# Residue-ordered query copies for the dilated heads, bias tables from memory, and gather buffers zeroed once

## The chip, the cores and the metric

The kernel runs on one core of one Trainium2 chip. The metric is the device time of one execution in microseconds (us), lower being better. The core's engines are TensorE (PE: matmuls, with its weight loads shown apart as PEld), VectorE (DVE), ScalarE (ACT), GpSimd (POOL) and SyncE (SP), which issues most of the DMAs. Each engine runs its own instructions in order and waits for the others by semaphores.

## The reference

One encoder block over 1024 tokens of width 1024: RMS norm, a combined projection to queries, keys and values, eight dilated heads and eight neighbourhood heads of width 64, an output projection, and a mixture of 16 experts with two chosen per token. What concerns the change is the dilated attention, whose bias depends on the head alone, and the gather of tokens for the experts:

```python
DIL_PATTERNS = ((128, 1), (512, 4), (2048, 16))

def dilated_window_attention(q, k, v, slopes, window, dilation):
    '''Centred dilated sliding window: query t attends to t + j*dilation, |j*dilation| <= window/2.
    Keys are gathered by stride: the sequence is split into `dilation` residue subsequences,
    each handled as a banded window of radius (window/2)/dilation over 64-query blocks.
    ...
    dist = (off * dilation).astype(jnp.float32)

    s = jnp.einsum('bhrnqd,bhrnkd->bhrnqk', qb, kb).astype(jnp.float32) * (HEAD_DIM ** -0.5)
    s = s - slopes[None, :, None, None, None, None] * dist
    s = jnp.where(valid, s, NEG_INF)
    ...

def dilated_mixture_attention(q, k, v, slopes):
    '''All (window, dilation) patterns per head, merged by their softmax denominators.'''
    results = [dilated_window_attention(q, k, v, slopes, w, d) for (w, d) in DIL_PATTERNS]
    ...
```

with slopes 2^-1, 2^-2, ... 2^-8 for the eight heads.

## The kernel before

Matmul operands are kept as two halves, a rounded high part (made by ScalarE, L103) and the remainder (made by VectorE or GpSimd, L104), and products are summed over the halves. The program goes through these stages, in the times of the profile: value projections (0 to 130 us); four pairs of dilated heads (130 to 345); four pairs of neighbourhood heads (345 to 480); the start of the output projection (480 to 545); its rest and the routing (545 to 620); the experts (620 to 892).

A pair of heads (class `Dil`, number `n` 0 to 3) has two heads `h`, and each head eight steps. Steps 0 to 3 are dense: the queries are 128 consecutive tokens. Steps 4 to 7 are residue steps: step 4 + r takes the tokens congruent to r modulo 4, in two halves z of 128 queries. The queries of a head lie as `q_s`, 128 partitions x 1024 tokens of 4 bytes, in the order of the tokens; the keys lie by residue already, since the evacuation that writes them (`k_hh`, L401) reads PSUM at a stride of 4. In `scores` (L411) the queries are the matmul's weights, so a residue step loads 128 weights with 16 bytes between them. Each half makes two matmuls (keys' high and low part), a step thus four: a score group.

The main loop (L852 on) goes through the steps s of all heads in one row, and the order in which it is written is the order on each engine. In step s it issues: the scores and biased softmax inputs of step s (`first`; `soft`, VectorE, L424); some projection matmuls of the next pair (`take`, L378, 96 in a pair, spread over its steps, the filling of TensorE); at step 1 and 2 of a pair the merge of the pair before (L578 among it); the transposes of step s-2 (`second`, L509) and their split into `pt_hi` (ScalarE) and `pt_lo` (VectorE); the exponentials of step s (`run_exps`, ScalarE, L430); up to two waiting evacuations of the projection (`run_slow(2)`: ScalarE L401, VectorE L402); at step 3 the store of the pair before (transposes of `ot`, L594); the value matmuls of step s-3 (`third`, L534 and L545), with `fold` (ScalarE, L438) and `ot` (VectorE, L440 or L442) after every second step. In residue steps `ot` is written at a stride of 4, in dense ones contiguously.

The biases of a head, 128 x 768, are made by GpSimd: at first `dist` and `mask` are loaded (`early_loads`, L459 and L460); for each head `prepare`, called in step 6 of the head before, halves `dist` (L465) and adds the mask to it (L466). GpSimd also splits weights (`w_lo`, L104). `early_loads` of the next head is called in step 1, and `late_loads` (the second copy `vb` of the values) in step 2.

For the experts, GpSimd gathers rows of tokens by an indirect DMA (`gather`, L1357) into the tiles `xg` and `xg1` (L1360); rows whose index is out of bounds are not written. The indices `gi` come from the routing.

Of the kernel before, what the change touches and what calls it, by code (L numbers as in the profile page):

```python
# [9 lines left out]
F32 = mybir.dt.float32  # L10
# [20 lines left out]
def shape_constants():  # L31

    p = np.arange(128)
# [11 lines left out]
    mask = -8 * np.concatenate([m_a, m_b], 1).astype(np.float32)  # L45

# [22 lines left out]
    return {"dist": dist, "mask": mask, "na_mask": na_mask, "ident": np.eye(128, dtype=np.float32),  # L69
# [3 lines left out]
def build(nc, tc, a, ctx, dbg=None):  # L73
# [71 lines left out]
    with ExitStack() as att:  # L145
# [15 lines left out]
        factors = qk.tile([128, 2], F32, name="factors", bufs=1)  # L161
# [11 lines left out]
        with ExitStack() as ph:  # L173
# [125 lines left out]
            nc.vector.memset(factors[:, 0:1], 0.5)  # L299
            nc.vector.memset(factors[:, 1:2], 8.0)  # L300
# [37 lines left out]
        class Pair:  # L338
# [70 lines left out]
            def scores(self, ps, h, qs, keys):  # L409
                for n, k in enumerate((self.kh, self.kl)):  # L410
                    nc.tensor.matmul(ps, self.q[h][:, qs], keys(k[h]), start=n == 0, stop=n == 1)  # L411
# [39 lines left out]
        class Dil(Pair):  # L451
# [3 lines left out]
            def early_loads(self, h):  # L455
                if self.n == 0 and h == 0:
                    Dil.dist = ap.tile([128, 768], F32, name="dist", tag="dist", bufs=1)
                    Dil.mask = ap.tile([128, 896], F32, name="mask", tag="mask", bufs=1)[:, :768]
                    nc.sync.dma_start(Dil.dist, a["dist"])  # L459
                    nc.sync.dma_start(Dil.mask, a["mask"])  # L460

            def prepare(self, h):
                head = 2 * self.n + h
                bias = self.bias[h] = ap.tile([128, 896], F32, name="bias", tag="bias")
                nc.gpsimd.tensor_tensor(Dil.dist, Dil.dist, factors[:, 0:1].to_broadcast([128, 768]), op=ALU.mult)  # L465
                nc.gpsimd.tensor_tensor(bias[:, :768], Dil.dist, Dil.mask, op=ALU.add)  # L466
# [7 lines left out]
            def late_loads(self, h):  # L474
                head = 2 * self.n + h
                vb = self.vb[h] = ap.tile([128, 8, 128], F32R, name="vb", tag="vb", bufs=1)
                nc.sync.dma_start(f(vb), vb_d[:, head * 128:(head + 1) * 128].rearrange("(k p) x -> p k x", p=128))

            def first(self, h, n):
# [4 lines left out]
                for z in range(2):  # L484
# [6 lines left out]
                    else:  # L491
                        r = n - 4
                        qs = slice(512 * z + r, 512 * z + r + 509, 4)
                        keys = lambda k: k[:, r * 256:r * 256 + 256]
                        todo.append((2 * r + z, 2, 512 - 128 * z))
                    self.scores(sp[:, 256 * z:256 * z + 256], h, qs, keys)
# [67 lines left out]
            def merge2(self):  # L564
# [5 lines left out]
                sb = ap.tile([128, 2, 2, 8], F32, name="sb")  # L570
                nc.vector.tensor_copy(sb.rearrange("p h z (q k) -> p k (h z) q", k=4),
                                      pb[:, 0:32].rearrange("p (k x q) -> p k x q", k=4, q=2))
                e = ap.tile([128, 2, 2, 8], F32, name="e")
# [793 lines left out]
    for e in range(2):  # L1367
        x0[e] = new_x()
        gather(x0[e], gi[:, 0, at(e)])
# [450 lines left out]
```

## Time and profile before

| | |
|---|---|
| median of 3 runs | 895.49 us (895.33 to 896.38) |
| profiled execution | 894.3 us |
| its span, first to last instruction | 892.5 us |
| mean granted clock of TensorE | 0.977 |
| busy in the span | PE 834.3 us (93%), DVE 565.1 (63%), ACT 512.6 (57%), POOL 234.4 (26%) |

A row of a timeline gives the start in microseconds from the span's start, the duration, the engine, the line, the operation, its output and inputs with their shapes, and in brackets how long the engine had been idle before and what ended that. Matmuls are pipelined: a row's duration is longer than what it adds, and what a row costs TensorE's queue is read from the start of the next. In a table by stage each engine has its busy time and its number of instructions in parentheses.

### The profile page before, as it was taken

The numbers are of one execution on the slowest core, as the hardware profiler recorded it, in microseconds if no ns is written. First come the engines' busy times: TensorE is split into PE (matmuls) and PEld (weight loads), VectorE is DVE, ScalarE is ACT, GpSimd is POOL, SyncE is SP. The second block draws the span as 40 slices with busy tenths as digits, with TensorE's granted clock in tenths as the row PEclk, the third lists the DMA queues.
The fourth block names the chain that finished last, engine by engine and source line by source line (L and its number), as shares of the span: only waits on it lengthen the run. The fifth ranks groups of instructions, "written<-read, shape, count | busy, mean of one in ns | idle before, by whom it ended". The sixth has DMA issues, their size and how long they took to land. (4 is left out here: it accounts for less than half of the span.)

```text
span 892.5 us, 13330 instructions
## 1 busy us (share of the span) xinstructions
PE 834.3 (93%) x4492; PEld 695.0 (78%) x4492; DVE 565.1 (63%) x1255; ACT 512.6 (57%) x1082; POOL 234.4 (26%) x187
## 2 busy tenths in 40 slices
PE   8999999999999999999898999999799999999962
PEld 5888878979889888878787887887677877777741
DVE  4551126776767767666677754677786566858693
ACT  5441127757667576677576623543585665857652
POOL 4001122221232202332310100000443343734553
PEclk8999999999999999999999999998999999999985
DMA  6865452314344141534447747995798987999743
GB/s 238 278 217 162 126 160 65 100 52 108 94 138 105 53 138 48 148 103 117 79 157 206 254 154 248 360 323 213 250 317 248 293 233 226 361 299 304 217 180 129
DMA packets 129919, 167.30 MB, mean 187 GB/s; under 512 B 15222, under 2 KB 101750, under 8 KB 129824
## 3 DMA queue, kind: packets, MB, share of 16 engines
q1 hardware_dynamic: 119616, 142.53, 49.6%
q0 software_dynamic: 10224, 23.79, 9.8%
q8 instruction: 41, 0.67, 0.3%
q14 instruction: 38, 0.31, 0.1%
HBM read 129.93 MB, written 47.47 MB: 199 GB/s over the span
## 5 line engine op out<-in xcount | busy, mean ns | idle before, releaser
L103 ACT ACTIVATE pt_hi<-ps_pt 128x512 fp32r<-128x512 f32 (+2 forms) x128 | 67.6, 528 | 70.6 <-PE ps_pt L509 41.5
L378 PE MATMUL ps_mm<-xhi,w_lo 128*128 128x512 f32 x256 | 105.1, 411 | 1.1 <-POOL w_lo L104 1.1
L378 PE MATMUL ps_mm<-xlo,w_hi 128*128 128x512 f32 x256 | 105.0, 410 | 0.0
L378 PE MATMUL ps_mm<-xhi,w_hi 128*128 128x512 f32 x256 | 102.9, 403 | 0.0
L104 POOL TENSOR_TENSOR w_lo<-w_raw,w_hi 128x1024 fp32r<-128x1024 f32 x16 | 38.3, 2394 | 229.3 <-ACT w_hi L103 229.3
L104 DVE TENSOR_TENSOR pt_lo<-ps_pt,pt_hi 128x512 fp32r<-128x512 f32 (+2 forms) x128 | 77.2, 603 | 31.8 <-ACT pt_hi L103 31.2
L424 DVE CUSTOM_DVE_ANT_0 p<-ps_s,bias 128x256 f32<-128x256 f32 (+1 forms) x192 | 81.8, 450 | 18.2 <-PE ps_s L411 10.8
L104 DVE TENSOR_TENSOR g_lo<-raw_up,g_hi 128x1024 fp32r<-128x1024 f32 x64 | 75.4, 1220 | 24.6 <-ACT g_hi L103 24.6
L1413 PE MATMUL ps_mm<-g_hi,x_hi 128*128 128x512 f32 x184 | 75.4, 410 | 0.9 <-ACT x_hi L103 0.9
L1413 PE MATMUL ps_mm<-g_hi,x_lo 128*128 128x512 f32 x184 | 74.0, 402 | 1.8 <-DVE x_lo L104 1.8
L1357 POOL DMA_INDIRECT xg<-hn_d,gi x32 | 44.3, 1383 | 118.0 <-ACT ge L1078 81.7
L1413 PE MATMUL ps_mm<-g_lo,x_hi 128*128 128x512 f32 x184 | 73.3, 398 | 0.0
L430 ACT ACTIVATE p<-p,stats 128x256 f32<-128x256 f32 x128 | 63.7, 500 | 9.7 <-DVE stats L424 9.5
L103 ACT ACTIVATE g_hi<-raw_up 128x1024 fp32r<-128x1024 f32 x64 | 64.3, 1067 | 0.9
L411 PE MATMUL ps_s<-k_hh,q_s 128*128 128x256 f32 (+1 forms) x192 | 60.7, 324 | 4.3 <-DMA k_hh<-k_hh 1.7
L411 PE MATMUL ps_s<-k_low,q_s 128*128 128x256 f32 (+1 forms) x192 | 62.6, 334 | 0.0
L411 PEld LDWEIGHTS ps_s<-k_hh,q_s 128*128 128x128 f32 x192 | 44.6, 232 | 11.2 <-DVE q_s L402 2.6
L378 PEld LDWEIGHTS ps_mm<-xhi,w_lo 128*128 128x128 f32 x256 | 48.7, 190 | 5.2 <-POOL w_lo L104 1.4
L378 PEld LDWEIGHTS ps_mm<-xhi,w_hi 128*128 128x128 f32 x256 | 48.7, 190 | 3.2
L378 PEld LDWEIGHTS ps_mm<-xlo,w_hi 128*128 128x128 f32 x256 | 48.5, 189 | 3.5
L411 PEld LDWEIGHTS ps_s<-k_low,q_s 128*128 128x128 f32 x192 | 44.7, 233 | 3.5
L430 ACT ACTIVATE p<-p,nm 128x384 f32<-128x384 f32 (+1 forms) x64 | 37.5, 586 | 14.4 <-DVE nm L424 14.0
(307 smaller groups left out, 2152.8 us busy)
## 6 DMA issues: line engine op xcount, KB each, us to landing
raw_up<-in_w_gate SPq DMA_DIRECT2D x32, 512.0 KB
raw_up<-in_w_up SPq DMA_DIRECT2D x32, 512.0 KB
raw_down<-in_w_down SPq DMA_DIRECT2D x16, 1024.0 KB
w_raw<-in_w_in SPq DMA_DIRECT2D x16, 512.0 KB
xt<-in_x SPq DMA_DIRECT2D x8, 512.0 KB
k_hh<-in_w_in SPq DMA_DIRECT2D x8, 512.0 KB
va_d<-vt SPq DMA_DIRECT2D x16, 256.0 KB
vb_d<-vt SPq DMA_DIRECT2D x8, 512.0 KB
```

The source lines that it names most:

```text
L103: nc.scalar.activation(hi, src, AF.Copy)
L104: (nc.gpsimd if pool else nc.vector).tensor_tensor(lo, src, f(hi), op=ALU.subtract)
L378: nc.tensor.matmul(ps, l[:, k, :], x[half][:, k, :], start=i == 0, stop=i == 23)
L411: nc.tensor.matmul(ps, self.q[h][:, qs], keys(k[h]), start=n == 0, stop=n == 1)
L424: nc.vector.tensor_tensor_reduce(out=p, in0=ps, in1=bias, scale=-0.125, scalar=3.0e38, op0=ALU.add, op1=ALU.min, accum_out=nm)
L430: nc.scalar.activation(p, p, AF.Exp, bias=nm, scale=-1.0, accum_out=l)
L1357: return nc.gpsimd.indirect_dma_start(out=x, out_offset=None, in_=src[:, :], in_offset=bass.IndirectOffsetOnAxis(ap=idx, axis=0), bounds_c ...
L1413: nc.tensor.matmul(ps, l[:, k, :], wt[:, k, :], start=i == 0, stop=i == 23)
```

## The change

1. Seven of the eight dilated heads (all but the second of pair 3) get a second tile `qr`, the queries ordered by residue. It is written by two ScalarE copies of 128 x 512 (`regroup`), two residues each, in steps 1 and 2 of the head, between the exponentials and `run_slow(2)`. In the residue steps of these heads `scores` takes its weights from `qr`, contiguously. `qr` uses the place of the former `mask`, with one buffer.
2. The biases come ready for each head from an input table, 8 x 128 x 768, loaded by `early_loads` in step 1 of the head before. The loads of `dist` and `mask` and GpSimd's sixteen operations for the biases are left out.
3. The four gather tiles are set to zero by GpSimd: two before the first two gathers, two after them.
4. Some small tiles of the merge have one buffer in place of two, and `na_mask` a longer place.

```diff
     m_b = np.where(mult == 0, BIG, np.where(mult == 2, -math.log(2.0), 0.0))
     dist = -8 * np.concatenate([d_a, 4 * d_i], 1).astype(np.float32)
     mask = -8 * np.concatenate([m_a, m_b], 1).astype(np.float32)
+    bias = np.stack([np.float32(0.5 ** (h + 1)) * dist + mask for h in range(8)])
 
     row, c8 = p // 8, p % 8
     start = np.clip(row - 4, 0, 8)
...
                 for h in range(2):
                     nc.sync.dma_start(f(self.kh[h])[own[1 - h], :], f(self.kh[h])[own[h], :])
 
-            def scores(self, ps, h, qs, keys):
+            def scores(self, ps, h, qs, keys, q=None):
                 for n, k in enumerate((self.kh, self.kl)):
-                    nc.tensor.matmul(ps, self.q[h][:, qs], keys(k[h]), start=n == 0, stop=n == 1)
+                    nc.tensor.matmul(ps, (self.q[h] if q is None else q)[:, qs], keys(k[h]), start=n == 0, stop=n == 1)
 
 
         slow = []
...
 
 
             def early_loads(self, h):
-                if self.n == 0 and h == 0:
-                    Dil.dist = ap.tile([128, 768], F32, name="dist", tag="dist", bufs=1)
-                    Dil.mask = ap.tile([128, 896], F32, name="mask", tag="mask", bufs=1)[:, :768]
-                    nc.sync.dma_start(Dil.dist, a["dist"])
-                    nc.sync.dma_start(Dil.mask, a["mask"])
+                bias = self.bias[h] = ap.tile([128, 896], F32, name="bias", tag="bias")
+                nc.sync.dma_start(bias[:, :768], a["bias"][2 * self.n + h])
 
             def prepare(self, h):
                 head = 2 * self.n + h
-                bias = self.bias[h] = ap.tile([128, 896], F32, name="bias", tag="bias")
-                nc.gpsimd.tensor_tensor(Dil.dist, Dil.dist, factors[:, 0:1].to_broadcast([128, 768]), op=ALU.mult)
-                nc.gpsimd.tensor_tensor(bias[:, :768], Dil.dist, Dil.mask, op=ALU.add)
 
                 va = self.v[h] = ap.tile([128, 11, 128], F32R, name="va", tag="va", bufs=1)
                 cols = slice(head * 128, (head + 1) * 128)
...
                 head = 2 * self.n + h
                 vb = self.vb[h] = ap.tile([128, 8, 128], F32R, name="vb", tag="vb", bufs=1)
                 nc.sync.dma_start(f(vb), vb_d[:, head * 128:(head + 1) * 128].rearrange("(k p) x -> p k x", p=128))
+
+            def grouped(self, h):
+
+                return (self.n, h) != (3, 1)
+
+            def regroup(self, h, half):
+
+                if half == 0:
+                    self.qr = ap.tile([128, 1024], F32R, name="qr", tag="mask", bufs=1)
+                rs = slice(2 * half, 2 * half + 2)
+                nc.scalar.activation(self.qr.rearrange("p (r i) -> p r i", r=4)[:, rs],
+                                     f(self.q[h]).rearrange("p (i r) -> p r i", r=4)[:, rs], AF.Copy)
 
             def first(self, h, n):
                 if n == 0 and h == 0:
...
                     else:
                         r = n - 4
                         qs = slice(512 * z + r, 512 * z + r + 509, 4)
+                        if self.grouped(h):
+                            qs = slice(256 * r + 128 * z, 256 * r + 128 * z + 128)
                         keys = lambda k: k[:, r * 256:r * 256 + 256]
                         todo.append((2 * r + z, 2, 512 - 128 * z))
-                    self.scores(sp[:, 256 * z:256 * z + 256], h, qs, keys)
+                    self.scores(sp[:, 256 * z:256 * z + 256], h, qs, keys,
+                                self.qr if n >= 4 and self.grouped(h) else None)
                 p = ap.tile([128, 512], F32, name="p", bufs=3)
                 for z, (t, s, b0) in enumerate(todo):
                     cols = slice(256 * z, 256 * z + 256)
...
                 for r in range(4):
                     nc.tensor.matmul(pb[:, 0:32], perm[:, 3 - r:131 - r], parts[:, :, :, 2 * r:2 * r + 2],
                                      start=r == 0, stop=r == 3)
-                sb = ap.tile([128, 2, 2, 8], F32, name="sb")
+                sb = ap.tile([128, 2, 2, 8], F32, name="sb", bufs=1)
                 nc.vector.tensor_copy(sb.rearrange("p h z (q k) -> p k (h z) q", k=4),
                                       pb[:, 0:32].rearrange("p (k x q) -> p k x q", k=4, q=2))
-                e = ap.tile([128, 2, 2, 8], F32, name="e")
-                nm = ap.tile([128, 2, 8], F32, name="nm2")
+                e = ap.tile([128, 2, 2, 8], F32, name="e", bufs=1)
+                nm = ap.tile([128, 2, 8], F32, name="nm2", bufs=1)
                 nc.vector.tensor_tensor(nm, st[:, :, 0, :], sb[:, :, 0, :], op=ALU.min)
                 nc.vector.tensor_tensor(e[:, 0], nm, st[:, :, 0, :], op=ALU.subtract)
                 nc.vector.tensor_tensor(e[:, 1], nm, sb[:, :, 0, :], op=ALU.subtract)
                 nc.scalar.activation(e, e, AF.Exp)
-                l2 = ap.tile([128, 2, 2, 8], F32, name="l2")
+                l2 = ap.tile([128, 2, 2, 8], F32, name="l2", bufs=1)
                 nc.vector.tensor_tensor(l2[:, 0], e[:, 0], st[:, :, 1, :], op=ALU.mult)
                 nc.vector.tensor_tensor(l2[:, 1], e[:, 1], sb[:, :, 1, :], op=ALU.mult)
                 nc.vector.tensor_tensor(nm, l2[:, 0], l2[:, 1], op=ALU.add)
...
                 q, g, m = steps[s - 2]
                 pts[s - 2] = q.second(g, m, ps.pop(s - 2))
             run_exps()
+            if s < 64 and n in (1, 2) and p.grouped(h):
+                p.regroup(h, n - 1)
             run_slow(2)
             take(s + 2 / 3)
             if before and at == 3:
...
 
     g_l = ex.tile([128, 1024], F32, name="g_l", bufs=1)
     bcast_row(g_l, a["norm_final_g"], 1024)
-    x0 = {}
+
+    x0, x1 = {}, {}
     for e in range(2):
         x0[e] = new_x()
+        nc.gpsimd.memset(x0[e], 0.0)
+    for e in range(2):
         gather(x0[e], gi[:, 0, at(e)])
+    for e in range(2):
+        x1[e] = new_x("xg1")
+        nc.gpsimd.memset(x1[e], 0.0)
 
     cnt = pos[:, 16 * (8 - LAST):16 * (9 - LAST)]
     V.tensor_copy(n_i[:, 0:16], cnt)
...
         return ex.tile([128, 256], F32, name="act", bufs=2)
 
     def second_gather(e):
-        x1[e] = new_x("xg1")
+        if e not in x1:
+            x1[e] = new_x("xg1")
         gather(x1[e], gi[:, 1, at(e)])
 
     def scatter(d, idx, src, **kw):
...
 
 
 
-    x1, xs, waiting, added = {}, {}, [], []
+    xs, waiting, added = {}, [], []
     spacer = ex.tile([128, 2], F32, name="spacer", bufs=1)[:, 0:1]
 
     def add_rows():
```

On ScalarE, at steps 1 and 2 of the second head of pair 0, the kernel before has this, with `pt_hi` the split of the transposes, `p` the exponentials, `k_hh` the evacuation of the next pair's keys:

```order
L103 ACTIVATE pt_hi<-ps_pt 128x512
L430 ACTIVATE p,stats<-p,stats 128x256 x2
L401 ACTIVATE k_hh<-ps_mm 64x4x128
L103 ACTIVATE pt_hi<-ps_pt 128x512
L430 ACTIVATE p,stats<-p,stats 128x256 x2
L401 ACTIVATE k_hh<-ps_mm 64x4x128
L438 ACTIVATE fold<-ps_o 64x512
L103 ACTIVATE pt_hi<-ps_pt 128x512
```

and the changed kernel this:

```order
L105 ACTIVATE pt_hi<-ps_pt 128x512
L431 ACTIVATE p,stats<-p,stats 128x256 x2
L483 ACTIVATE qr<-q_s 128x512
L402 ACTIVATE k_hh<-ps_mm 64x4x128
L105 ACTIVATE pt_hi<-ps_pt 128x512
L431 ACTIVATE p,stats<-p,stats 128x256 x2
L483 ACTIVATE qr<-q_s 128x512
L402 ACTIVATE k_hh<-ps_mm 64x4x128
L439 ACTIVATE fold<-ps_o 64x512
L105 ACTIVATE pt_hi<-ps_pt 128x512
```

Each of two evacuations, and with them the fold behind the second, now has a copy ahead of it.

On ScalarE, at steps 0 to 3 of the first head of pair 1, with `e` the merge of pair 0 and `fold` that of its last step, before:

```order
L103 ACTIVATE pt_hi<-ps_pt 128x512
L430 ACTIVATE p,stats<-p,stats 128x256 x2
L578 ACTIVATE e<-e 128x32
L103 ACTIVATE pt_hi<-ps_pt 128x512
L430 ACTIVATE p,stats<-p,stats 128x256 x2
L438 ACTIVATE fold<-ps_o 64x512
L103 ACTIVATE pt_hi<-ps_pt 128x512
```

and after:

```order
L105 ACTIVATE pt_hi<-ps_pt 128x512
L431 ACTIVATE p,stats<-p,stats 128x256 x2
L483 ACTIVATE qr<-q_s 128x512
L588 ACTIVATE e<-e 128x32
L105 ACTIVATE pt_hi<-ps_pt 128x512
L431 ACTIVATE p,stats<-p,stats 128x256 x2
L483 ACTIVATE qr<-q_s 128x512
L439 ACTIVATE fold<-ps_o 64x512
L105 ACTIVATE pt_hi<-ps_pt 128x512
```

The first copy stands ahead of the merge's `e`, the second ahead of the fold.

On GpSimd, where the experts begin (`acc_d` is set to zero there; `n_i` is the table of counts, read into a register), before:

```order
L760 DMA acc_d<-k_hh 128x1024 x6
L1357 DMA xg<-hn_d,gi 128x1024 x2
L1380 TENSOR_LOAD n_i
L1357 DMA xg<-hn_d,gi 128x1024
L1357 DMA xg_6711<-hn_d,gi 128x1024
L1357 DMA xg_6715<-hn_d,gi 128x1024
```

and after:

```order
L770 DMA acc_d<-k_hh 128x1024 x6
L1382 MEMSET xg 128x1024 x2
L1369 DMA xg<-hn_d,gi 128x1024 x2
L1387 MEMSET xg_6580 128x1024
L1387 MEMSET xg_6582 128x1024
L1398 TENSOR_LOAD n_i
L1369 DMA xg<-hn_d,gi 128x1024
L1369 DMA xg_6580<-hn_d,gi 128x1024
L1369 DMA xg_6582<-hn_d,gi 128x1024
```

Two memsets have come ahead of the first two gathers, and two between them and the reading of the counts.

## Rows read from the trace of the kernel before

**Rows 1.** Busy time by stage, here the dilated stage (start:end, length, engines, clock, DMA, GB/s)
```profile
130.00:345.00 215.00, 207.51 (x1279) 183.59 (x1278) 147.43 (x425) 146.66 (x390) 53.39 (x32) 1.00 0.34 94
```

**Rows 2.** TensorE's timeline around a score group of a residue step
```profile
175.34 0.28 PE L411 MATMUL ps_s<-k_hh,q_s 128*128 128x256 f32 x1
...
176.16 0.40 PE L378 MATMUL ps_mm<-xhi,w_lo 128*128 128x512 f32 x1
```

**Rows 3.** TensorE's timeline around a score group of a dense step
```profile
157.01 0.28 PE L411 MATMUL ps_s<-k_hh,q_s 128*128 128x256 f32 x1
...
157.48 0.40 PE L378 MATMUL ps_mm<-xhi,w_hi 128*128 128x512 f32 x1
```

**Rows 4.** Line 411, its weight loads: count, duration in ns min/median/max
```profile
L411 PEld LDWEIGHTS ps_s<-k_hh,q_s x192: 186/188/335, 130.8 to 517.2; 128*128 128x128 f32 x192
```

**Rows 5.** TensorE's timeline, the residue group behind the store's transposes
```profile
195.19 0.48 PE L411 MATMUL ps_s<-k_hh,q_s 128*128 128x256 f32 x1
...
196.21 0.39 PE L378 MATMUL ps_mm<-xhi,w_hi 128*128 128x512 f32 x1
```

**Rows 6.** The page's groups, a contiguous ScalarE copy (busy us, mean ns)
```profile
L103 ACT ACTIVATE g_hi<-raw_up 128x1024 fp32r<-128x1024 f32 x64 | 64.3, 1067 | 0.9
```

**Rows 7.** Line 401 in the dilated stage, ScalarE reading PSUM (ns min/median/max)
```profile
L401 ACT ACTIVATE q_s<-ps_mm x14: 574/592/593, 131.3 to 295.6; 64x512 fp32r<-64x512 f32 x14
L401 ACT ACTIVATE k_hh<-ps_mm x14: 574/586/595, 147.8 to 313.8; 64x512 fp32r<-64x512 f32 x14
```

**Rows 8.** Line 442 in the dilated stage, VectorE's ot (ns min/median/max)
```profile
L442 DVE TENSOR_TENSOR ot<-ps_o,fold x26: 681/686/1092, 144.8 to 317.6; 64x512 f32<-64x512 f32 x26
```

**Rows 9.** ScalarE's timeline, second head of pair 0, steps 1 to 3
```profile
160.49 0.57 ACT L401 ACTIVATE k_hh<-ps_mm 64x512 fp32r<-64x512 f32 x1
...
162.15 0.51 ACT L430 ACTIVATE p<-p,stats 128x256 f32<-128x256 f32 x1 [0.35 <-DVE stats L424]
...
163.27 0.59 ACT L401 ACTIVATE k_hh<-ps_mm 64x512 fp32r<-64x512 f32 x1
...
164.50 0.60 ACT L103 ACTIVATE pt_hi<-ps_pt 128x512 fp32r<-128x512 f32 x1
```

**Rows 10.** VectorE's timeline of the same steps
```profile
164.62 1.09 DVE L442 TENSOR_TENSOR ot<-ps_o,fold 64x512 f32<-64x512 f32 x1
...
166.24 0.67 DVE L104 TENSOR_TENSOR pt_lo<-ps_pt,pt_hi 128x512 fp32r<-128x512 f32 x1
```

**Rows 11.** TensorE's timeline, the value matmul that reads the last pt_lo
```profile
167.63 0.28 PE L534 MATMUL ps_o<-pt_lo,va 128*128 128x256 f32 x1
```

**Rows 12.** ScalarE's timeline, first head of pair 1, steps 1 to 3
```profile
188.70 0.23 ACT L578 ACTIVATE e<-e 128x32 f32<-128x32 f32 x1 [1.58 <-DVE e L577]
...
190.42 0.59 ACT L438 ACTIVATE fold<-ps_o 64x512 f32<-64x512 f32 x1
```

**Rows 13.** TensorE's timeline, the store's transposes of ot
```profile
192.17 0.33 PE L594 MATMUL ps_o<-ident,ot 128*128 128x128 f32 x1 [0.20 <-DVE ot L442]
```

**Rows 14.** Lines 465 and 466, GpSimd's bias operations (ns min/median/max)
```profile
L465 POOL TENSOR_TENSOR dist<-dist,factors x8: 1457/1470/1492, 119.6 to 310.5; 128x768 f32<-128x768 f32 x8
...
L466 POOL TENSOR_TENSOR bias<-dist,mask x8: 1832/1838/1859, 121.1 to 312.1; 128x768 f32<-128x768 f32 x8
```

**Rows 15.** SyncE's timeline, two DMA issues
```profile
116.04 0.35 SPq L459 DMA_DIRECT2D dist<-in_dist  x1
...
617.70 0.33 SPq L127 DMA_DIRECT2D g_l<-in_norm_final_g  x1
```

**Rows 16.** GpSimd's timeline, the first bias operation and the gathers
```profile
119.59 1.47 POOL L465 TENSOR_TENSOR dist<-dist,factors 128x768 f32<-128x768 f32 x1 [17.61 <-DMA dist<-in_dist]
...
624.30 1.08 POOL L1357 DMA_INDIRECT xg<-hn_d,gi  x1 [81.67 <-ACT ge L1078]
...
630.15 1.05 POOL L1357 DMA_INDIRECT xg<-hn_d,gi  x1 [3.44 <-PE ps_pt L1401]
```

**Rows 17.** Line 171, GpSimd's memsets (ns min/median/max)
```profile
L171 POOL MEMSET k_low<- x4: 944/945/950, 1.3 to 4.3; 64x1024 f32 x4
```

More of the change, by code (lines that the diff above doesn't have):

```diff
@@ L68, in shape_constants @@
     small[:, 56] = 1024 + p
-    return {"dist": dist, "mask": mask, "na_mask": na_mask, "ident": np.eye(128, dtype=np.float32),
+    return {"bias": bias, "na_mask": na_mask, "ident": np.eye(128, dtype=np.float32),
             "tri": tri, "iota": iota, "small": small, "perm": perm, "zeros": np.zeros((128, 372), np.float32)}
@@ L159, in split_w @@
             return hi, lo
-        factors = qk.tile([128, 2], F32, name="factors", bufs=1)
+        factors = qk.tile([128, 1], F32, name="factors", bufs=1)
         perm = qk.tile([128, 136], F32, name="perm", bufs=1)
@@ L298, in build @@
                 v_store(T, v_out(ps))
-            nc.vector.memset(factors[:, 0:1], 0.5)
-            nc.vector.memset(factors[:, 1:2], 8.0)
+            nc.vector.memset(factors, 8.0)
             nc.sync.dma_start(perm, a["perm"])
@@ L609, in early_loads @@
                     if self.n == 0:
-                        Nbr.mask = ap.tile([128, 896], F32, name="na_mask", tag="mask", bufs=1)
+                        Nbr.mask = ap.tile([128, 1024], F32, name="na_mask", tag="mask", bufs=1)[:, :896]
                         nc.sync.dma_start(Nbr.mask, a["na_mask"])
@@ L617, in prepare @@
                 if h == 0:
-                    nc.gpsimd.tensor_tensor(self.nb, self.nb, factors[:, 1:2, None].to_broadcast([128, 2, 384]),
+                    nc.gpsimd.tensor_tensor(self.nb, self.nb, factors[:, :, None].to_broadcast([128, 2, 384]),
                                             op=ALU.mult)
```

## The prediction

> **What bounds the kernel now.** I read the busy shares by stage first, because the edits of the attention loop and the two late ones lie in different stages. In the dilated stage, 130 to 345 us, TensorE is busy 207.51 of 215.00 us, ScalarE 146.66, VectorE 147.43, GpSimd 53.39, and the DMA engines 34% of the time [rows 1]. So a microsecond off TensorE's queue is a microsecond off the stage, work on GpSimd or in a DMA is worth nothing unless TensorE ends up waiting for it, and work added to ScalarE has about 68 us of idle time in sum, but costs where it stands in a chain that TensorE waits for. I then read single stretches: TensorE's rows around score groups with strided and with contiguous queries, and ScalarE's, VectorE's and TensorE's rows at the two places into which the copies go.
>
> **Strided scores, removed.** A score group is four matmuls that load 128 queries each as weights. In a residue step the queries lie 16 bytes apart, and the group holds TensorE from 175.34 to 176.16, 0.82 us [rows 2]. In a dense step, with contiguous queries and the same 256 columns, it takes 157.01 to 157.48, 0.47 us [rows 3]. The weight loads show why: 0.186 us at the least and 0.335 at the most [rows 4]. The trace has 32 strided groups; all but the four of the last head become contiguous. Three of the 28 stand right behind the store's transposes and take 1.02, from 195.19 to 196.21 [rows 5]; there no contiguous group can be seen, and I take 0.45 off, between 0.35 and 1.02 - 0.47 = 0.55. So 25 x 0.35 + 3 x 0.45 = 10.1 us come off TensorE. This is the whole gain of the change.
>
> **The copies, added.** Fourteen ScalarE copies of 128 x 512, two per head in steps 1 and 2, reading the queries at stride 4 and writing contiguously. No row of before is a ScalarE read of the on-chip buffer at a stride, so their price c is bounded. From below by contiguous copies: 128 x 1024 takes 1.067 us, so half is 0.53 [rows 6]. ScalarE's stride-4 reads of PSUM cost no more than its contiguous ones (k_hh 586 ns strided, q_s 592 contiguous) [rows 7], which speaks for the low end. From above by strided access to the same memory: VectorE's ot takes 0.681 us at the least, written contiguously, and 1.092 at the most, written at this stride [rows 8], 0.41 more for 512 elements; the weight loads pay 0.335 - 0.186 = 0.149 us more per 128 columns [rows 4], 0.60 for 512. So c lies between 0.53 and 0.53 + 0.60 = 1.13. I take 0.53 + 0.41 = 0.94, an engine's read or write of 512 elements being nearer to a copy than a weight load is.
>
> A rule can be weighed here. The row is the strided weight load that takes 1.8 times the contiguous one [rows 4]. The Trainium skill, "SBUF — State Buffer", section "Door 1: The DMA port swizzle", says that each access which crosses to a new 16-byte line pays a penalty, but also that one can stride for free up to 4 fp32 elements. The stride here is just that, and the two halves of the rule part: by the second, c would be 0.53 and the forecast that of the fast copy below; by the first, c is dearer. The weight load and ot agree with the first half, so I keep 0.94; no row of before shows it for ScalarE.
>
> **What of the copies lies on the path.** Two places repeat.
>
> Second heads (pairs 0, 1, 2). ScalarE runs k_hh, pt_hi, exponentials, k_hh, fold, pt_hi from 160.49 to 165.10, with no gap over 0.35 us [rows 9]; behind it VectorE does k_low, ot at 164.62, two softmaxes, and pt_lo at 166.24 [rows 10]. Both copies stand ahead of those, so the chain comes 2c later. That pt_lo ends at 166.24 + 0.67 = 166.91 and is needed by TensorE's value matmul at 167.63 [rows 11], which leaves 0.72 us; but TensorE itself gets there 0.35 earlier, its strided group just before being shorter, so 0.37 is left. Stall: 2c - 0.37 for each of three heads.
>
> First heads (pairs 1, 2, 3). The first copy falls into ScalarE's 1.58 us of idle before the merge's exponential at 188.70 and is free. The second stands ahead of fold at 190.42 [rows 12]; fold releases ot and that the transposes at 192.17, which wait for it 0.20 us already [rows 13]. So there is no slack. Stall: c for each of three heads. The first head of pair 0 has no such store, and its chain has room: nothing.
>
> Sum: -10.1 + 3(2c - 0.37) + 3c = 9c - 11.2. At c = 0.94: **-2.7 us**. At 0.53: -6.4; at 1.13: -1.0.
>
> **Bias tables.** Removed: 8 x (1.470 + 1.838) = 26.5 us of GpSimd [rows 14], which no engine waited for. Nothing gets shorter. Added: a 384 KB load per head, asked for in step 1 of the head before; the first load of dist, of the same size, landed 119.59 - 116.04 = 3.6 us after its issue, when GpSimd's wait for it ended [rows 15, 16], and a head lasts 215 / 8 = 27 us [rows 1], so it is there some 20 us early, with DMA two thirds idle. It stands ahead of the vb load in SyncE's queue and waits for the last softmax of the head before, done by then: vb is delayed by one issue. 0 us. If the load were late, its head's first softmax would wait; at 3.6 us of 27 this has no chance worth pricing.
>
> **Gather buffers.** Four GpSimd memsets; the one kind in the trace is 0.945 us for 64 x 1024 [rows 17], and with all 128 partitions I take the same, since rows run side by side. GpSimd idles 81.67 us before the first gather at 624.30; a load that waits for the same memory to come free is issued at 617.70 [rows 15, 16], so two memsets (1.9 us) can be over by 619.6, long before the indices come. The other two fit into the 3.44 us idle before the gather at 630.15. 0 us; up to 1.9 if the first pair has to wait for a buffer that comes free only with the indices. The smaller tiles move nothing.
>
> **Result.** The profiled execution of 894.3 us becomes 894.3 - 2.7 = 891.6, and the median, 895.49, which lies 1.2 above it, becomes **892.8**. What this kernel's measurement can tell from no change is about 0.2%, 1.8 us: under 893.7 is faster, over 897.3 slower.
>
> **Rivals.**
> 1. The copies are fast: c = 0.53, as ScalarE's PSUM reads have it: -6.4, 889.1. (The rule weighed above, from the Trainium skill, would give this by its second half.) Were they also to fit beside other work, the full -10.1 would show: 885.4. Against it stand the strided weight load and ot.
> 2. The copies eat the gain: c = 1.13 or more, or stalls that also delay the next step: -1.0, 894.5, and up to c = 1.44 no measurable change.
> 3. Slower: ScalarE becomes the bound of steps 1 and 2. The mechanism is the same chain (copy, k_hh, fold, ot, pt_lo, value matmuls); it decides from c = 11.2 / 9 = 1.24 on, and shows beyond 1.44. At c = 1.5, nearly three times what a contiguous read costs, it is +2.3, 897.8. For it: the chain from 160.49 to 165.10 is nearly full. Against it: neither strided row costs that much more.
> 4. The change doesn't do what it says: the contiguous weight loads stay slow, being read from another tile. Then only the stalls remain, 9c - 1.1 = +7.4, 902.9. The dense steps read the same kind of tile fast, so hardly.
> 5. The first memsets hold up the first gather: +1.9 on the forecast, 894.7.
>
> **How the numbers follow.** Forecast (c from 0.80 to 1.04, that is -4.0 to -1.8): 0.42. Fast copy: 0.22. Gain eaten: 0.23. Memsets late, on the forecast: 0.04, same. Slower by the chain: 0.07; change without effect: 0.02. Faster 0.42 + 0.22 = 0.64, same 0.27, slower 0.09. The range goes from below the fast copy, -7.3 (some stalls hidden), to the point where the copies have eaten the gain, +0.4: 888.2 to 895.9; what is left out, about 0.2, is the full gain below and the slower side above.
>
> **What the profile after would show.** Weight loads from qr of 0.19 us and score groups of 0.47 in residue steps, with only four of 0.82 left; fourteen ScalarE rows qr of 0.94 us; TensorE's rows with idle before the value matmuls of steps like 167.63 of about 1.5 us in three heads and before the transposes of ot of about 1.1 in three; the stage from 130 to 345 shorter by 2.7, and the stages behind it of the same length. Wrong would be: copies far from 0.94, idle before TensorE where none is named here, or the first gather starting later against its indices.

## The result, and the profile after

The changed kernel takes 897.54 us (median of 20 runs, 895.6 to 902.44), the kernel before 893.81 beside it (20 runs, 890.98 to 896.65). The ratio, taken over all the runs and not from the two medians, is 1.0051 with a 95% interval of 1.0039 to 1.0064: 4.6 us slower (3.5 to 5.7; the medians alone are 3.7 apart), where 2.7 us faster was forecast and 895.9 was the upper end of the range. The profiled execution of the changed kernel, 902.44 us with a span of 900.7, is the longest of its twenty: what its profile shows says where the time goes, and the sizes there are those of this one execution.

The dilated stage, as in [rows 1]:

```profile
130.00:345.00 215.00, 200.16 (x1261) 174.03 (x1259) 144.94 (x423) 158.74 (x398) 30.54 (x18) 0.98 0.37 102
```

TensorE is busy 7.4 us less in the same 215 us, but that is idle time, not work done sooner: from the first score matmul (131.07 us before, 129.92 after) to the last value matmul of the dilated heads (353.13 and 355.41) the stage takes 225.49 us in place of 222.06. It has become 3.4 us longer, and the granted clock in it is 0.98 on the mean, where it was 1.00.

The tile `qr` (line, engine, operation, count, nanoseconds min/median/max), against [rows 4] and the price c of the copies:

```profile
L412 PEld LDWEIGHTS ps_s<-k_hh,qr x56: 187/188/337, 139.0 to 319.9; 128*128 128x128 f32 x56
...
L483 ACT ACTIVATE qr<-q_s x14: 1101/1118/1140, 136.6 to 303.6; 128x512 fp32r<-128x512 f32 x14
```

The weight loads are contiguous and take 0.188 us: the change does what it says. The copies take 1.118 us, near the upper bound of 1.13 and not the 0.94 that was taken. What TensorE waited for between 130 and 345 us (in total, times, longest), after and before:

```profile
PE ps_o L544 <- DVE pt_lo L106: 4.2, 3, 1.4
PE ps_o L604 <- DVE ot L443: 3.4, 3, 1.2
```

```profile
PE ps_o L594 <- DVE ot L442: 0.4, 2, 0.2
```

Before, the first of these waits is not there and the second is 0.2 us at most. Both stand where the prediction put them, three times each: 1.4 us where 2c - 0.37 gives 1.87, and 1.2 (0.2 of it there before) where c gives 1.12. Then comes what the prediction does not have. TensorE's rows behind the first stall:

```profile
166.45 0.39 PE L544 MATMUL ps_o<-pt_lo,va 128*128 128x256 f32 x1 [1.41 <-DVE pt_lo L106]
...
168.25 0.63 PE L379 MATMUL ps_mm<-xhi,w_lo 128*128 128x512 f32 x1
168.68 0.63 PE L379 MATMUL ps_mm<-xhi,w_hi 128*128 128x512 f32 x1
...
171.24 0.40 PE L379 MATMUL ps_mm<-xlo,w_hi 128*128 128x512 f32 x1
171.48 0.27 PE L412 MATMUL ps_s<-k_hh,qr 128*128 128x256 f32 x1
```

The projection matmul of 512 columns at 168.25 holds TensorE for 0.43 us, the one at 171.24 for 0.24. The stretches ahead, in and behind show why (start:end, length, busy time of PE, PEld, DVE, ACT and POOL, granted clock, DMA share, GB/s). The last two rows are two more stretches at half clock, behind a wait for ot and behind another wait for pt_lo:

```profile
164.40:167.80 3.40, 1.99 (x14) 1.65 (x13) 2.68 (x10) 2.52 (x7) 0.20 (x1) 1.00 0.37 78
167.90:171.20 3.30, 3.30 (x12) 2.75 (x12) 2.23 (x7) 2.66 (x8) 2.08 (x1) 0.50 0.01 4
171.30:174.70 3.40, 3.40 (x27) 3.13 (x26) 2.49 (x7) 2.68 (x10) 0.00 (x0) 1.00 0.50 147
195.20:198.50 3.30, 3.30 (x15) 2.95 (x14) 2.16 (x6) 0.00 (x0) 2.59 (x3) 0.50 0.26 79
280.50:283.80 3.30, 3.30 (x13) 2.83 (x12) 1.66 (x3) 2.25 (x7) 2.38 (x1) 0.50 0.00 0
```

From 167.83 to 171.24 the granted clock is 0.50, the lower of the two levels (1.2 GHz), though TensorE has no gap in it; in the stretch ahead it was idle for 1.41. The profile of the kernel before has no stretch at half clock between 130 and 345 us.

The second loss is where the experts begin. GpSimd's memsets, then two VectorE operations beside them, of after and of before:

```profile
623.53 1.85 POOL L1382 MEMSET xg<- 128x1024 f32 x2 [77.36 <-DVE tmp L1078]
...
629.95 1.85 POOL L1387 MEMSET xg<- 128x1024 f32 x2
```

```profile
623.78 2.13 DVE L1124 TENSOR_SCALAR d_hi<-iota,pk 128x256 bf16<-128x256 bf16 x4
...
629.17 2.68 DVE L1101 CAST wb<-w 128x16 bf16<-128x16 f32 x1
```

```profile
621.64 0.88 DVE L1112 TENSOR_SCALAR d_hi<-iota,pk 128x256 bf16<-128x256 bf16 x4
...
625.66 0.24 DVE L1089 CAST wb<-w 128x16 bf16<-128x16 f32 x1
```

Four d_hi take 2.13 us in place of 0.88, the second cast of `wb` 2.68 in place of 0.24, and the cast ends as the memsets beside it do (631.85 and 631.80 us). TensorE waits for them, after and before:

```profile
625.52 0.71 PE L1132 MATMUL ps_o<-feat,d_hi 128*128 128x48 bf16 x8 [1.75 <-DVE d_hi L1124]
...
632.92 0.21 PE L1132 MATMUL ps_o<-feat,d_hi 128*128 128x48 bf16 x2 [2.18 <-DVE feat L1105]
```

```profile
621.99 0.81 PE L1120 MATMUL ps_o<-feat,d_hi 128*128 128x48 bf16 x8 [0.35 <-DVE d_hi L1112]
...
626.97 0.21 PE L1120 MATMUL ps_o<-feat,d_hi 128*128 128x48 bf16 x2 [0.89 <-DVE feat L1093]
```

Its waits there grow by 1.40 and 1.29 us, and both VectorE operations lie on the way from the routing to the experts' weights: 1.25 and 2.44 us, 3.7 together. From its first matmul on `feat` to its last TensorE takes 11.1 us in place of 7.3. The first gather, on the other hand, is no later against its indices: it starts 1.02 us behind the operation that makes them (626.53 to 627.55), before 1.20 (623.10 to 624.30).

The first pair of memsets did not begin at 617.70, when the load of `g_l`, which waits for the same memory, was issued before [rows 15]. The store of the tokens and that load after, and the store before:

```profile
618.10 0.32 SPq L1223 DMA_DIRECT2D hn_d<-hn  x1
623.36 0.33 SPq L129 DMA_DIRECT2D g_l<-in_norm_final_g  x1
```

```profile
614.83 0.32 SPq L1211 DMA_DIRECT2D hn_d<-hn  x1
```

The load goes out 5.3 us behind the store in this execution and 2.9 before, and the memsets begin 0.17 us behind it, beside d_hi. That both wait for the store to land is inferred. In the other profiles the same distance is 2.8 us, 3.5 or 5.0, and 5.0 in two kernels without memsets too, so it is not the memsets that make it long; what does is not shown.

The span of this profile is 8.1 us longer than that of before: 3.4 us in the dilated stage, 3.8 on the way to the experts' weights, and 0.9 in sum in the other stages, where executions differ by as much.

### The profile page after: what moved, and what is told of

It reads as the page before. It is cut to its first block, busy times and chain, and to the rows that moved or that the text cites. A ratio compares the mean times of both kernels' runs of the same rounds, so it can differ in the third digit from the quotient of the medians.

```text
span 900.7 us, 13341 instructions
## 1 busy us (share of the span) xinstructions
PE 826.2 (92%) x4492; PEld 686.4 (76%) x4492; DVE 569.5 (63%) x1254; ACT 527.3 (59%) x1096; POOL 208.5 (23%) x175
## 5 line engine op out<-in xcount | busy, mean ns | idle before, releaser
L1369 POOL DMA_INDIRECT xg<-hn_d,gi x32 | 41.2, 1287 | 38.7 <-PEq L1546 9.3
L443 DVE TENSOR_TENSOR ot<-ps_o,fold 64x512 f32<-64x512 f32 x36 | 30.8, 855 | 24.9 <-ACT fold L439 24.4
L412 PE MATMUL ps_s<-k_hh,q_s 128*128 128x256 f32 (+1 forms) x136 | 41.3, 314 | 4.9 <-DMA k_hh<-k_hh 2.1
L1431 PEld LDWEIGHTS ps_mm<-g_hi,x_lo 128*128 128x128 f32 x184 | 35.3, 192 | 12.8 <-DVE x_lo L106 4.1
L403 DVE TENSOR_TENSOR k_low<-ps_mm,k_hh 64x512 fp32r<-64x512 f32 x32 | 22.0, 688 | 35.9 <-ACT k_hh L402 35.9
```

What stands on the lines that cost most here:

```text
L403: low.append(lambda hi=hi, lo=lo, src=src: nc.vector.tensor_tensor(lo, src, f(hi), op=ALU.subtract))
L412: nc.tensor.matmul(ps, (self.q[h] if q is None else q)[:, qs], keys(k[h]), start=n == 0, stop=n == 1)
L443: nc.vector.tensor_tensor(dst, view(ps[0:64, :]), view(t), op=ALU.add)
L1369: return nc.gpsimd.indirect_dma_start(out=x, out_offset=None, in_=src[:, :], in_offset=bass.IndirectOffsetOnAxis(ap=idx, axis=0), bounds_c ...
L1431: nc.tensor.matmul(ps, l[:, k, :], wt[:, k, :], start=i == 0, stop=i == 23)
```

## The experiments

Two theories for the 4.6 us stood against each other. A: the memsets hold VectorE up and cost most of it, while the copies' stalls and the half-clock stretches behind them just eat the shorter score groups. B: the copies cost it all. All kernels were timed beside the kernel before. The microseconds are the ratio applied to the median of before. In the table "stage" is the time from the first dilated score matmul to the last value matmul against 222.06 before, in the profiled execution, and "half clock" the number of stretches at 0.50 in it.

| kernel | ratio to before (95%) | us | stage, us | half clock |
|---|---|---|---|---|
| changed kernel | 1.0051 (1.0039 to 1.0064) | +4.6 | +3.4 | 3 |
| no_zero | 1.0015 (1.0001 to 1.0028) | +1.3 | +6.1 | 5 |
| zero_tables | 1.0036 (1.0019 to 1.0053) | +3.2 | 0.0 | 0 |
| tables_only | 0.9999 (0.9984 to 1.0015) | -0.1 | 0.0 | 0 |
| no_copy | not comparable | | -9.7 | 0 |
| copy_unused | 1.0073 (1.0047 to 1.0099) | +6.5 | +8.6 | 1 |
| spare | 0.9996 (0.9979 to 1.0013) | -0.4 | -0.5 | 1 |
| spare2 | 1.0005 (0.9982 to 1.0028) | +0.4 | -0.7 | 0 |
| placed | 0.9877 (0.9855 to 0.9899) | -11.0 | -9.1 | 1 |
| gpsimd_copy | 0.9943 (0.9921 to 0.9965) | -5.1 | -6.7 | 1 |
| placed_zero | 0.9871 (0.9848 to 0.9893) | -11.5 | -9.5 | 0 |
| placed_memset | 0.9929 (0.9907 to 0.9952) | -6.3 | -9.5 | 0 |

### One part at a time

**no_zero** leaves the memsets out:

```diff
     for e in range(2):
         x0[e] = new_x()
-        nc.gpsimd.memset(x0[e], 0.0)
...
-    for e in range(2):
-        x1[e] = new_x("xg1")
-        nc.gpsimd.memset(x1[e], 0.0)
```

> The changed kernel without the four memsets. Theory A (the memsets hold VectorE up: its d_hi row of four takes 2.13 us beside a memset and 0.88 before, a cast 2.68 against about 0.2, together 3.7 us on the path from the routing to the first gathers, while the copies' stalls and half-clock stretches just eat the 10.1 us of the shorter score groups): 3.7 us less than the changed kernel, within 1 us of the kernel before. Theory B (the copies with their stalls and the clock cost all of the 3.7 us, and what the memsets delay is made up later): as slow as the changed kernel, +3 to +4 us on before.

**zero_tables** has `grouped` return False: no copies. **tables_only** has neither copies nor memsets.

> The changed kernel without the residue copies (queries strided as before), with tables and memsets. Theory A: +3.7 us on before, d_hi and the cast long as in the changed kernel. Theory B: within 1 us of before.

> The bias tables alone: no copies, no memsets. Both theories: within 0.5 us of before, no VectorE operation changed by GpSimd's 26.5 us less work. If GpSimd's bias operations had slowed VectorE or the loads delayed a head: visibly faster or slower, some us.

The parts add up: memsets 3.2 us (1.7 to 4.7), copies 1.3 (0.1 to 2.5), tables -0.1, in sum 4.4 of 4.6. Theory A holds, B falls. In zero_tables the first pair of memsets came early, and only the second met an operation that it held up:

```profile
617.52 1.86 POOL L1382 MEMSET xg<- 128x1024 f32 x2 [75.20 <-DVE a_f L982]
...
625.10 1.85 POOL L1387 MEMSET xg<- 128x1024 f32 x2
```

```profile
620.19 0.88 DVE L1124 TENSOR_SCALAR d_hi<-iota,pk 128x256 bf16<-128x256 bf16 x4
...
624.65 2.34 DVE L1103 CAST wb<-w 128x16 bf16<-128x16 f32 x1
```

d_hi is 0.88 us again, the third cast 2.34. In all three profiles with memsets on GpSimd (this one, the changed kernel, placed_memset below) the second pair costs; the first costs in the two in which it came late enough to meet d_hi. The first pair of zero_tables did not run alone: beside it VectorE's tensor_tensor, scalar_tensor_tensor and reductions kept their length (two `b_at` 0.36 us, as before). So a memset does not hold up all that VectorE does. From TensorE's first matmul on `feat` to its last, the three take 9.8 us (zero_tables), 11.1 and 10.4, and every kernel without memsets on GpSimd 7.3 to 7.6.

The price of the copies varies from execution to execution: the profiled execution of no_zero, 897.6 us where the median of its runs is 894.3, has five stretches at half clock, two of them:

```profile
167.20:170.50 3.30, 3.30 (x13) 2.81 (x12) 1.92 (x5) 2.39 (x7) 2.38 (x1) 0.50 0.00 0
...
252.40:255.80 3.40, 3.40 (x16) 3.06 (x15) 2.50 (x7) 0.27 (x1) 2.21 (x2) 0.50 0.23 70
```

The mean granted clock of its twelve runs has a median of 0.9745, against 0.981 of the runs before beside it.

### The gain and the price of the copies by themselves

**no_copy** takes contiguous slices of the queries as they lie and never calls `regroup`; **copy_unused** calls it and takes the strided slices of the kernel before. Both read `q_s`:

```diff
-                                self.qr if n >= 4 and self.grouped(h) else None)
+                                None)
```

> The scores take their weights contiguously from the queries as they lie (the wrong tokens), so the copies are left out, and so are the memsets; tables as in the changed kernel. Both theories: no stall of 1.4 us before the value matmuls, no half-clock stretch between 130 and 345 us, and -10 us on before. If TensorE then waits for the softmax chain in the residue steps instead, less: -5 to -8.

> The changed kernel without memsets in which the copies are made but not read: the scores take the strided queries as before, so no score group is shorter, and what is left is the copies' price alone. The stalls are then 1.4 - 0.35 = 1.06 us before the value matmuls and 1.0 before the store's transposes, three of each with 0.3 us of slower restart: 7 us. Theory A (half-clock stretches behind the stalls add to them): +10 to +14 on before, with three or more stretches between 130 and 345 us. Without a price of the clock: +6 to +8.

The gain is 9.7 us in the stage, without a half-clock stretch (10.1 was predicted). The whole of no_copy can't be compared: it computes with other queries, and its total is 17.3 us lower, 7.6 more than the stage; that its tokens then go to other experts is the likely reason and is not shown. The price of the copies alone, in copy_unused:

```profile
PE ps_o L542 <- DVE pt_lo L106: 3.6, 3, 1.2
PE ps_o L602 <- DVE ot L443: 3.4, 3, 1.2
```

The waits grow by 3.6 and 3.0 us. With a slower restart behind each of the six (in the changed kernel 0.22 us from 166.45 to the next matmul, where the one at 167.63 before takes 0.12) and one stretch at half clock the stage is 8.6 longer. Three stretches or more and +10 to +14 in all were expected, so this was a miss: with 1.2 us of stall in place of 1.4 the clock fell behind one of six, and the +6.5 in all is what was expected of stalls without a price of the clock.

### Is it the idle time that lowers the clock?

**spare** puts spare matmuls in front of the two waits, their results overwritten:

```diff
+                    if half == 0 and h == 1 and self.n < 3:
+                        for _ in range(10):
+                            nc.tensor.matmul(op[:, 0:256], self.v[h][:, 0, :], pt[0][:, 0:2, :],
+                                             start=True, stop=True, skip_group_check=True)
                     m = 0
                     for c, s0, w in todo:
...
                     pn = bank("o")
+                    if half == 0 and z == 1 and self.n < 3:
+                        for _ in range(10):
+                            nc.tensor.transpose(pn[:, 0:128], ident, ident)
```

> As the changed kernel without memsets, with ten spare matmuls of 256 columns ahead of the value matmuls that wait for pt_lo, and ten spare transposes ahead of the store's transposes that wait for ot (three places each; their results are overwritten). They lie in the idle time, 1.2 to 1.4 us, so without a clock effect nothing changes. Theory A (TensorE's idle makes the granted clock fall to half for a stretch behind it, 1.4 us lost each, three to five times): no half-clock stretch between 130 and 345 us, 4 to 7 us less than the same kernel without spare matmuls, -3 to -6 on before. Rival C (the half-clock stretches have another cause): they stay, within 1 us of the kernel without spare matmuls.

TensorE's waits for ot and pt_lo in it:

```profile
PE ps_o L608 <- DVE ot L443: 2.2, 2, 1.2
...
PE ps_o L548 <- DVE pt_lo L106: 1.1, 3, 0.4
```

The idle time before the value matmuls was filled, that before the store was not: the spare transposes wrote the PSUM bank that ot was still reading, and at two of three places in the stage waited themselves. Neither of these two waits has a stretch at half clock behind it. The one that is left, from 186.0, stands behind waits for q_s and the merge (0.78 and 0.62 us; 0.53 and 0.61 before). In all, -3 to -6 us were expected and -0.4 came. **spare2** gives the transposes a bank of the scores:

```diff
-                            nc.tensor.transpose(pn[:, 0:128], ident, ident)
+                            nc.tensor.transpose(spare[:, 0:128], ident, ident)
```

> As the kernel with spare matmuls, but the ten spare transposes ahead of the store's transposes go to another PSUM bank, since in the first attempt they waited for ot themselves (the bank was released by it). Now both kinds of idle time are filled. Theory A: the waits for pt_lo and for ot are under 0.4 us each, no half-clock stretch behind them, the dilated stage 0.6 to 1 us shorter than before, -2 to 0 on before and a mean clock as before. If the spare transposes delay the chain instead: +1 to +3.

```profile
PE ps_o L612 <- DVE y L614: 2.7, 3, 0.9
...
PE ps_o L548 <- DVE pt_lo L106: 1.1, 3, 0.4
```

The granted clock from 150 to 345 us (last figure but two), of no_zero and of spare2:

```profile
150.00:345.00 195.00, 182.18 (x1128) 158.81 (x1126) 132.96 (x383) 140.40 (x355) 28.05 (x17) 0.96 0.39 108
```

```profile
150.00:345.00 195.00, 187.42 (x1227) 164.15 (x1226) 137.00 (x396) 145.54 (x368) 28.19 (x17) 1.00 0.40 111
```

No stretch at half clock is left between 130 and 345 us, and the stage is 0.7 us shorter than before, though the copies stand where they do in no_zero, where it is 6.1 longer. TensorE only does something while it waits. The difference, 6.8 us over five stretches, is 1.36 us each, and the changed kernel's three give 1.37. By the total, spare2 is only 0.9 us under no_zero, and these intervals do not show that the two totals differ: the profiled execution of no_zero is 3.3 us over the median of its runs, so a common one has fewer stretches than five.

### Another place, another engine

**placed** moves the same fourteen copies behind the fold of a step, with a tile for each half of the residues:

```diff
+        places = {(0, 1): [(0, 0)], (0, 4): [(0, 1)], (0, 6): [(1, 0)], (1, 0): [(1, 1)]}
...
-            if s < 64 and n in (1, 2) and p.grouped(h):
-                p.regroup(h, n - 1)
...
                 q.third(g, m, pts.pop(s - 3))
+            copies(s)
             take(s + 1)
```

(head and step, then the head and half that is copied there; no memsets.)

> As the changed kernel without memsets, but with the fourteen ScalarE copies at other places, behind the fold of a step: residues 0 and 1 of a first head in its step 1, 2 and 3 in its step 4; of a second head in step 6 of the first and in its own step 0 (two tiles of half the size). ScalarE has 0.85 to 1.6 us of idle in those steps. Theory A (the copies cost by their place in the chain fold, ot, pt_lo, and by the clock behind the stalls): no stall, no half-clock stretch in the dilated stage, -9 to -10 on before. Rival D (15.7 us more work on ScalarE is the price): within 3 us of before.

```profile
L485 ACT ACTIVATE qra<-q_s x7: 1110/1128/1137, 137.5 to 289.8; 128x512 fp32r<-128x512 f32 x7
```

```profile
PE ps_o L606 <- DVE y L608: 2.0, 3, 0.9
...
PE ps_o L557 <- DVE pt_lo L106: 0.5, 2, 0.3
...
PE ps_o L606 <- DVE ot L443: 0.2, 1, 0.2
```

The copies take as long as in the changed kernel, 1.128 us, and nobody waits for them: 9.1 us off the stage, where no copies at all take 9.7 off, and 11.0 in all. ScalarE's 15.7 us more work cost next to nothing; their place did. One stretch at half clock is left, at 237.1 to 240.5, behind waits for q_s and the merge, which the kernel before has too (the first is up to 0.2 us longer here).

**gpsimd_copy** leaves the copies where they were and gives them to GpSimd (`nc.gpsimd.tensor_copy`):

> As the changed kernel without memsets, the fourteen copies made by GpSimd at the same places in the program. ScalarE's chain is then as before. If GpSimd holds VectorE up in a copy as in a memset: VectorE operations of 1 to 2 us beside each copy, the chain late by about as much, -4 to +1 on before. If it holds it up in memsets only: -9 to -10.

```profile
L483 POOL CAST qr<-q_s x14: 1087/1117/1127, 132.6 to 290.5; 128x512 fp32r<-128x512 f32 x14
```

GpSimd takes the same 1.117 us, and the kernel is 5.1 us faster than before (3.1 to 7.1), a little outside the -4 to +1 that was expected. pt_lo, the softmax and the evacuations, which read PSUM, keep their length; one operation, with all its operands in the on-chip buffer, does not (with the copies, and before):

```profile
L568 DVE TENSOR_TENSOR parts<-stats,perm x8: 211/220/1015, 183.6 to 343.3; 128x64 f32<-128x64 f32 x8
```

```profile
L558 DVE TENSOR_TENSOR parts<-stats,perm x8: 218/220/228, 186.3 to 350.1; 128x64 f32<-128x64 f32 x8
```

```profile
PE ps_pt L578 <- DVE parts L568: 3.8, 3, 1.4
```

`parts`, 0.22 us, takes up to 1.015 where a copy runs, three times, and TensorE waits 3.8 us for it where it waited 1.5. These 2.3 us and one stretch at half clock cover the 2.8 us by which its stage gains less than that of placed_zero below (and 0.9 more, given back elsewhere).

**placed_zero** keeps the new places and has ScalarE zero the gather tiles (a copy with scale 0), **placed_memset** GpSimd as in the changed kernel:

```diff
-        nc.gpsimd.memset(x0[e], 0.0)
+        nc.scalar.activation(x0[e], ident[:, 0:1].to_broadcast([128, 1024]), AF.Copy, scale=0.0)
```

> The copies as in the kernel with other places, and the four gather tiles zeroed by ScalarE (which waits 9.5 us for VectorE there), two ahead of the first gathers and two behind the exponentials of the weights. Theory A (the memsets cost because they hold VectorE): d_hi 0.9 us for four again, within 1 us of the kernel with other places, -8 to -10 on before. If zeroing costs by the gathers that wait for it: -5 to -7.

> The copies at the better places, with the four GpSimd memsets of the changed kernel. Theory A (the memsets hold VectorE operations on the path, whatever comes before): a cast of 2 us or more beside the second pair, d_hi of 0.9 or 2.1 us for four according to whether the first pair is over, +2.5 to +3.7 on the kernel with other places, -7 to -8 on before. If the memsets' price came from the late attention stage: as fast as without them, -10.

placed_zero also has a one-column exponential ahead of its first pair, and its second pair stands behind the exponentials of the weights; neither is tested by itself. ScalarE and VectorE of placed_zero, then VectorE of placed_memset:

```profile
608.75 2.00 ACT L1394 ACTIVATE xg<-ident 128x1024 f32<-128x1024 f32 x2 [3.48 <-DVE e L1021]
613.34 0.23 ACT L1100 ACTIVATE ge<-ge 128x32 f32<-128x32 f32 x1 [2.59 <-DVE ge L1098]
...
613.57 1.99 ACT L1414 ACTIVATE xg<-ident 128x1024 f32<-128x1024 f32 x2
```

```profile
610.91 0.88 DVE L1134 TENSOR_SCALAR d_hi<-iota,pk 128x256 bf16<-128x256 bf16 x4
...
614.96 0.18 DVE L1111 CAST wb<-w 128x16 bf16<-128x16 f32 x1
```

```profile
610.49 1.85 DVE L1134 TENSOR_SCALAR d_hi<-iota,pk 128x256 bf16<-128x256 bf16 x4
...
615.91 2.35 DVE L1113 CAST wb<-w 128x16 bf16<-128x16 f32 x1
```

Zeroing on ScalarE falls into its idle time and leaves d_hi at 0.88 us and the casts at 0.18; on GpSimd they are 1.85 and 2.35 again. placed_memset is 4.7 us slower than placed, more than the 2.5 to 3.7 expected, though their two intervals allow 1.9 to 7.5. placed_zero does all that the changed kernel does and has the lowest ratio of those that do, 1.3% under the kernel before; it and placed can't be told apart.

## Why the prediction was wrong

Two steps failed, the memsets taken at 0 and a stall taken for its length only, and one term was mis-sized, c. Between the forecast of -2.7 and the measured +4.6 lie 7.3 us. By the totals 3.2 of them are the memsets; 9 x (1.118 - 0.94) = 1.6 are the price of the copies; the remaining 2.4 (no_zero's +1.3 against -1.1 from the sum at the measured c) are of the copies too, and in the profiles the half-clock stretches stand there.

- **The memsets** were costed at 0 on the ground that GpSimd was idle and the gathers were late enough. Both are true, and neither is what mattered: a running memset holds up VectorE's tensor_scalar and cast. The step looked for who waits for the memset's result, and not for what the running memset holds. The rival that came nearest had 1.9 us and another mechanism, a late first gather; measured were 3.2 (1.7 to 4.7). The Trainium skill has the rule, in "SBUF — State Buffer", section "Who interferes with whom": copy, cast and tensor_scalar on VectorE can contend with GpSimd for a shared port pair when their operands meet certain conditions, whoever issues first gets it for the whole instruction, and the other fully blocks. By the same section a tensor_tensor with both inputs in the buffer contends with a GpSimd operation that reads the buffer, not with one that only writes it. The traces agree on what is held up: tensor_scalar (d_hi, 2.13 for 0.88) and cast (2.68 for 0.24) beside a memset, tensor_tensor (`parts`, 1.015 for 0.22) beside a copy but not beside a memset. On the order they agree for d_hi, whose row begins behind the memset's. For the cast they don't: in all three profiles its row begins 0.45 to 0.78 us ahead of the memset's and still ends with the second memset.
- **The clock** was not in the sum at all. The step that failed is the one that took a stall for its length only: "a microsecond off TensorE's queue is a microsecond off the stage" leaves out that a stretch of 3.4 us at half clock can stand behind a stall. Three cost 4.1 us in the profile of the changed kernel, which turns -0.7 into +3.4. That is the longest execution of twenty; by the totals no more than the 2.4 us above are left for the clock and all else.
- **The price of a copy** was mis-sized: c is 1.118 us, not 0.94, at the end of the bounds that the weight loads gave. With it the sum 9c - 11.2 is -1.1 where -2.7 stood. The Trainium skill, "SBUF — State Buffer", section "Door 1: The DMA port swizzle", lets 4 fp32 elements be strided for free. The measured copy at that stride takes 2.1 times half of [rows 6], so that half of the rule does not hold for ScalarE here.
- **The gain** was right: 10.1 us predicted, 9.7 measured without copies.
- **The stalls** were right in place. Their sum, 9c - 1.1 or 9.0 us at the measured c, came out too, since the stage without half-clock stretches (spare2, -0.7) against no_copy (-9.7) gives 9.0; but this is in part luck. The waits themselves grew by 7.2 (1.4 us in place of 1.87 before the value matmuls), six slower restarts are some 0.6, and what the other 1.2 are is not shown.
- **The tables** were right at 0 (-0.1 us, -1.4 to 1.3).
- **The slower rival** had c from 1.44 on as its condition. c stayed under that, and it was slower all the same, by two mechanisms on no list. The sum of the rival without effect was wrong by its own rows: with strided groups TensorE gets no sooner to the value matmuls, so 0.72 us of slack are left and not 0.37, and 9c - 1.1 should be 9c - 2.2.

What stays open: what decides whether a stall is followed by a half-clock stretch. The same stalls had three in one execution and five in another, stalls of 1.2 us had one, and placed has one without a new stall. That filling the idle time removes them is shown by one pair of profiles and by the mean clocks (0.9745 without spare work, 0.9795 with it), and not by the totals. Nor is it shown what the changed kernel's median execution, as against the profiled one, pays for the clock.

## What to carry to other kernels

A copy that an idle engine could do for nothing costs up to its full length if it stands ahead of a link of the chain that the bound engine waits for: place it by the chain, step by step, and not by the engine's busy share (from +1.3 to -11.0 us here, with the same copies). Cost a stall of TensorE with a stretch at half clock that may stand behind it. And before an engine off the path is given work, ask not only who waits for it, but which operations of another engine cannot run while it runs.

## What the runs showed of the hardware

- ScalarE and GpSimd read the on-chip buffer at a stride of 16 bytes at the same price, 1.12 us for 128 x 512, while ScalarE's reads of PSUM at a stride cost nothing more [rows 7].
- A stretch of 3.41 us at half clock (167.83 to 171.24) costs an estimated 1.36 us in a stage that TensorE bounds (6.8 us over five stretches, 4.1 over three, by the differences between three executions).
- Two GpSimd memsets of 128 x 1024 take 1.85 us, 0.93 each, like the 64 x 1024 of [rows 17]; ScalarE zeroes two of the same tiles in 2.00.
